# SwiGLU first projections: the seven-product scheme over latent tokens and context together, in halves of 384 tokens

## The chip, the cores and the metric

The kernel runs on one core of a Trainium2 chip. The metric is the device time of one execution in microseconds. A core has a matrix engine (PE, with its weight loads listed apart as PEld), a vector engine (DVE), an activation engine (ACT), a general engine (POOL) and a queue that issues most of the loads (SP).

## The reference, cut to what matters

A trunk of two layers works on 512 latent tokens (x) and 256 context tokens (ctx) of width 1024. Each layer holds two SwiGLU blocks with a mixer between them; the last block of the last layer is done for x alone.

```python
def swiglu(x, w13, w2):
    a, b = jnp.split(x @ w13, 2, axis=-1)          # w13: 1024 x 5632
    return (jax.nn.silu(a) * b) @ w2               # w2: 2816 x 1024
...
    for l in range(DEPTH):
        x = x + 0.5 * ml[2] * swiglu(modulate(x, norm_g[l, 0], ml[0], ml[1]), ffn_w13[l, 0], ffn_w2[l, 0])
        ctx = ctx + 0.5 * mc[2] * swiglu(modulate(ctx, norm_g[l, 0], mc[0], mc[1]), ffn_w13[l, 0], ffn_w2[l, 0])
        ...
        x = x + 0.5 * ml[8] * swiglu(modulate(x, norm_g[l, 2], ml[6], ml[7]), ffn_w13[l, 1], ffn_w2[l, 1])
        if not last:
            ctx = ctx + 0.5 * mc[8] * swiglu(modulate(ctx, norm_g[l, 2], mc[6], mc[7]), ffn_w13[l, 1], ffn_w2[l, 1])
```

## The kernel before, in words

Activations lie transposed, features on the 128 partitions and tokens along the free axis. Every product of the projections is done in split precision: each operand is held as a rounded high part and a low part (`xnhx`, `xnlx` for x, `xnhc`, `xnlc` for the context, `whi`, `wlo` for weights), and `mmk` (L367) issues three matmuls per 128x128 weight tile: high by high (L369), low activation by high weight (L371), high activation by low weight (L373).

There are four SwiGLU blocks, built by `ffn_steps` (L517): f0, f1, f2 for x and context, f3 for x alone. The 2816 hidden features are 22 steps of 128. A plain step (`up`, L559) multiplies eight tiles of the gate half and eight of the value half with 512 columns of x and 256 of the context: 48 matmuls of 512 columns and 48 of 256. Later steps are "fast" ones (`up_fast`, L635): from step 3 on in f0, f2 and f3, from step 18 on in f1, so 19 + 4 + 19 steps with context and 19 without.

A fast step treats the product as a 2x2 block product: the input features in two halves of 512 (four tiles each), the output as gate and value, the 512 tokens of x in two halves of 256. A Strassen-Winograd scheme then needs seven block products (a11, a12, s1, s2, s3, s4, a22) in place of eight, with sums of weight quarters (`fast_job`, L567, on POOL, L576 to L582) and sums of activation quarters. The context takes no part in the scheme: it is multiplied plainly with the four raw quarters a11, a12, a21, a22 of the weights (tile `sc`), which is why a21 is split and kept although the scheme for x does not need it. A step has 7 x 12 matmuls of 256 columns for x and 4 x 12 of 256 for the context.

The activation sums are made once per block by `fast_sums` (L607), called four times (k = 0 to 3) at the places that the tables `FP0` to `FP3` name: in the middle of the first projections of the context, at their end ("e"), or at the end of a given plain step. Per call DVE does seven adds of 256 columns (L615 to L621) and the low part of two sums (L364), POOL three adds and a low part (L612 to L614, L624), ACT the high parts (L363, L623). Sums lie in two tiles `xt0`, `xt1`; the fourth sum `t4` waits in a temporary until `fast_prep2` (L627) writes it over the second half of the lower four tiles of `xnhx`, `xnlx`, just before the first fast step.

Order of the work: each engine runs its instructions in the order in which the program emits them. Weights come by SP into three raw buffers of 2048 columns; `advance` (L128) splits a job into pieces (high part on ACT, L162; low part on DVE, or on POOL for piece s1, L163) as long as fewer than eight pieces are out, and a raw buffer is loaded anew when its last piece has been split. In a fast step each block product gives its piece back by itself (`relc`), and the next piece is split there. The second projections (`down`) come between the fast steps, two steps' features at a time; they add their result to `hT` on DVE (`resid`, L688), which frees the PSUM bank. PSUM has seven banks for products, taken in turn by `PS`.

Of the kernel before, what the change touches and what calls it, by code (L numbers as in the profile page):

```python
# [9 lines left out]
F32 = mybir.dt.float32  # L10
F32R = mybir.dt.float32r
# [3 lines left out]
ALU = mybir.AluOpType  # L15
# [44 lines left out]
def trunk_kernel(  # L60
# [31 lines left out]
    ones = const.tile([P, P], F32, name="ones")  # L92
    nc.vector.memset(ones, 1.0)
# [151 lines left out]
    acc = np_.tile([P, NT + 8], F32, name="acc")  # L245
    rst = np_.tile([P, NT + 8], F32, name="rst")
# [270 lines left out]
    def ffn_steps(l, fi, zf, zt, nxt, parts=PARTS, rest=None, fast=0, prep=(), delay=False):  # L517
# [68 lines left out]
        FORD = ["a11", "a12"] + ["a21"] * both_zs + ["s1", "s2", "s3", "s4", "a22"]  # L586

        def fast_open():
            T["xt"] = tuple(open_pool(f"xt{i}").tile([P, 3, 4, NH], F32R, name=f"xt{i}") for i in range(2))

        def fast_close():
            for i in (1, 0):
                close_pool(f"xt{i}")

        def fast_prep(at):

            for k in [i for i, z in enumerate(prep) if fast and z == at]:
                if k == 0:
                    if (l, fi) == (0, 1):
                        T["drain"]()  # L600
                    fast_open()
                    T["t4"] = [tmp.tile([P, 2, NH], F32, tag="rs_m", name="t4") for _ in range(2)]
                fast_sums(k)

        def fast_sums(k):
            xh, xl = T["xnx"]
            th, tl = T["xt"]  # L607
            q = lambda t, k, h: t[:, k, h * NH:h * NH + NH].bitcast(F32)
            a0, a1, b0, b1 = [(q(xh, k + i, h), q(xl, k + i, h)) for i in (0, 4) for h in range(2)]
            t = tmp.tile([P, SAW], F32, tag="sa", name="tsum")[:, :3 * NH].rearrange("p (i n) -> p i n", i=3)  # L610
            t1, t2, t3, t4 = t[:, 0], t[:, 1], t[:, 2], T["t4"][k // 2][:, k % 2]
# [8 lines left out]
            V.tensor_tensor(t4, b0[0], t2, ALU.subtract)  # L620
            V.tensor_tensor(t4, t4, b0[1], ALU.add)  # L621
            split(th[:, 0:2, k], tl[:, 0:2, k], t[:, 0:2])
            SC.activation(th[:, 2, k], t3, AF.Copy)  # L623
            GP.tensor_tensor(tl[:, 2, k], t3, th[:, 2, k].bitcast(F32), ALU.subtract)  # L624

        def fast_prep2():
            xh, xl = T["xnx"]  # L627
            for i in range(2):
                s = slice(2 * i, 2 * i + 2)
                split(xh[:, s, NH:], xl[:, s, NH:], T["t4"][i])  # L630

        def up_fast(j):
            def fn(w):
                gslot = slot(j)
                xh, xl = T["xnx"]  # L635
                th, tl = T["xt"]
                gh, gl = T["g"]
                s0, s1, s2 = (slice(i * NH, i * NH + NH) for i in range(3))
                pa, pb, pc, pd = (PS(f"s{i}") for i in range(4))
                cc = PS("sc") if both_zs else None  # L640

                def prod(name, ps=None, x=None, half=None, k0=0):

                    wh, wl = w.parts[FORD.index(name)]
                    ws = [(wh[:, hs(k)], wl[:, hs(k)]) for k in range(4)]
                    for k in range(4 if x else 0):
                        mmk([(ps, *x(k))], ws[k], k == 0, k == 3)
                    for k in range(4 if both_zs and half is not None else 0):
                        mmk([(cc[:, half * NCTX:half * NCTX + NCTX], *xk("c", k0 + k))], ws[k], k0 + k == 0, k0 + k == KD - 1)
                    T["relc"](name != "a22")  # L650
                xq = lambda i, s: lambda k: (xh[:, i + k, s], xl[:, i + k, s])
                xt = lambda i: lambda k: (th[:, i, k], tl[:, i, k])
                sa = tmp.tile([P, SAW], F32, tag="sa", name="sa")
                u = tmp.tile([P, NX], F32, tag="rs_m", name="u")
# [5 lines left out]
                prod("a11", pa[:, s0], xq(0, s0), 0)  # L660
                prod("a12", pa[:, s1], xq(4, s0), 0, 4)
                SC.copy(sa[:, s2], pa[:, s0])
                V.tensor_tensor(sa[:, s0], pa[:, s1], sa[:, s2], ALU.add)
                if both_zs:
                    prod("a21", half=1)
                prod("s1", pb[:, s1], xt(0))
                prod("s2", pb[:, s0], xt(1))
                SC.activation(sa[:, s0], sa[:, s0], AF.Silu)
                V.tensor_tensor(u[:, s0], pb[:, s0], sa[:, s2], ALU.add)
                V.tensor_tensor(u[:, s1], pb[:, s1], u[:, s0], ALU.add)  # L670
                prod("s3", pc[:, s1], xt(2))
# [1615 lines left out]
```

## Time and profile before

| | |
|---|---|
| time, median of 3 runs | 2989.99 us (2988.91 to 2992.88) |
| the profiled execution | 2993.55 us |
| its span, first to last instruction | 2991.8 us |
| PE busy | 2832.5 us (95%), 21247 matmuls |
| DVE busy | 2005.1 us (67%) |
| ACT, POOL busy | 1112.4 us (37%), 1087.0 us (36%) |
| mean granted clock of TensorE | 0.963 of full |

Spans count from the first instruction. A busy time counts the union of an engine's instructions; matmuls overlap in the records, so what one costs in a row of many is read from start to start. The block f0 lies at about 65 to 600 us, f1 at about 1330 to 1860, f2 at about 1870 to 2420, f3 at about 2620 to 2980.

### The profile page before, as it was taken

The page shows a single profiled execution, that of the slowest core. Times are in us where ns is not written, and L with a number is a line of the kernel's source. Part 1 is how long each engine was busy: PE and PEld are TensorE (multiplying, and loading weights), DVE is VectorE, ACT ScalarE, POOL GpSimd, SP SyncE. Part 2 cuts the span into 40 slices and gives each one's busy share as a digit, 9 for nine tenths or more (in the row PEclk, how much of TensorE's full clock was granted, in tenths as well). Part 3 has the DMA queues.
Part 4 walks back from the last instruction along what each step waited for, and adds up shares of the span by engine and source line. Part 5 has one row for each costly group of instructions (what it writes and reads, how often), then busy time and mean ns, then how long its engine had stood idle before and what let it go on. Part 6 is the DMA issues. An engine that isn't in the chain of part 4 may idle for free.

```text
span 2991.8 us, 53430 instructions
## 1 busy us (share of the span) xinstructions
PE 2832.5 (95%) x21247; PEld 2520.0 (84%) x21247; DVE 2005.1 (67%) x3817; ACT 1112.4 (37%) x2311; POOL 1087.0 (36%) x1232
## 2 busy tenths in 40 slices
PE   7899999998997899999999999999999989899998
PEld 5799999977885677888888889799999977678997
DVE  4665666667857667658666576766666656588887
ACT  4233333343444435432222233433333332344444
POOL 0242333339307833002655232443333300046653
PEclk9899999998897898999999999999999989899999
DMA  6323341221234584332333211122221226433331
GB/s 228 104 73 127 99 127 57 65 72 43 75 106 158 200 261 150 128 83 76 105 101 103 99 54 54 50 71 62 67 76 60 71 66 211 162 105 100 113 99 64
DMA packets 306104, 308.34 MB, mean 103 GB/s; under 512 B 35053, under 2 KB 261513, under 8 KB 299200
## 3 DMA queue, kind: packets, MB, share of 16 engines
q1 hardware_dynamic: 284592, 274.89, 28.8%
q10 hardware_dynamic: 20256, 25.76, 2.6%
q8 instruction: 167, 2.74, 0.4%
q0 software_dynamic: 1008, 4.29, 0.4%
q14 instruction: 81, 0.66, 0.1%
HBM read 279.34 MB, written 25.56 MB: 102 GB/s over the span
## 4 chain that ended last, share of the span: by engine, by line
PE 73%; DVE 13%; ACT 4%; DMA 2%; POOL 2%; issue 2%; SPq 0%; ACTq 0%; POOLq 0%; DVEq 0%
PE s L369 7%; PE s L373 7%; PE s L371 7%; PE sc L371 3%; PE sc L369 3%; PE sc L373 3%; DVE wlo L163 2%; PE b L1266 1%; DVE nt L321 1%; DVE hT L688 1%; PE uac L373 1%; PE uac L371 1%; PE uac L369 1%; PE uax L369 1%; PE uax L371 1%
## 5 line engine op out<-in xcount | busy, mean ns | idle before, releaser
L163 DVE TENSOR_TENSOR wlo<-raw,whi 128x512 fp32r<-128x512 f32 (+1 forms) x793 | 596.1, 787 | 300.3 <-ACT whi L162 287.5
L162 ACT ACTIVATE whi<-raw 128x512 fp32r<-128x512 f32 (+1 forms) x813 | 476.0, 617 | 687.7 <-PE sc L371 122.4
L369 PE MATMUL s<-xnhx,whi 128*128 128x256 f32 x976 | 277.0, 284 | 0.0
L371 PE MATMUL s<-xnlx,whi 128*128 128x256 f32 x976 | 276.3, 283 | 0.4 <-DVE xnlx L364 0.4
L373 PE MATMUL s<-xnhx,wlo 128*128 128x256 f32 x976 | 276.2, 283 | 0.0
L659 POOL TENSOR_TENSOR gl<-sa,gh 128x256 fp32r<-128x256 f32 x122 | 95.8, 805 | 331.0 <-ACT gh L658 331.0
L373 PE MATMUL s<-xt,wlo 128*128 128x256 f32 x732 | 207.4, 283 | 1.8 <-POOL wlo L163 1.8
L369 PE MATMUL s<-xt,whi 128*128 128x256 f32 x732 | 207.1, 283 | 0.0
L371 PE MATMUL s<-xt,whi 128*128 128x256 f32 x732 | 207.1, 283 | 0.0
L578 POOL TENSOR_TENSOR raw<-raw 128x512 f32<-128x512 f32 x61 | 82.1, 1346 | 311.8 <-issue 286.5
L369 PEld LDWEIGHTS s<-xnhx,whi 128*128 128x128 f32 x976 | 187.2, 192 | 7.6 <-DVE hT L688 3.4
L369 PE MATMUL sc<-xnhc,whi 128*128 128x256 f32 x672 | 190.2, 283 | 0.0
L371 PE MATMUL sc<-xnlc,whi 128*128 128x256 f32 x672 | 190.2, 283 | 0.0
L373 PE MATMUL sc<-xnhc,wlo 128*128 128x256 f32 x672 | 190.1, 283 | 0.0
L371 PEld LDWEIGHTS s<-xnlx,whi 128*128 128x128 f32 x976 | 187.2, 192 | 1.5 <-DVE xnlx L364 0.6
L373 PEld LDWEIGHTS s<-xnhx,wlo 128*128 128x128 f32 x976 | 187.2, 192 | 0.0
L373 PEld LDWEIGHTS s<-xt,wlo 128*128 128x128 f32 x732 | 140.5, 192 | 2.0 <-POOL wlo L163 2.0
L369 PEld LDWEIGHTS s<-xt,whi 128*128 128x128 f32 x732 | 140.5, 192 | 0.0
L371 PEld LDWEIGHTS s<-xt,whi 128*128 128x128 f32 x732 | 140.5, 192 | 0.0
L369 PEld LDWEIGHTS sc<-xnhc,whi 128*128 128x128 f32 x672 | 129.0, 192 | 0.0
L371 PEld LDWEIGHTS sc<-xnlc,whi 128*128 128x128 f32 x672 | 129.0, 192 | 0.0
L373 PEld LDWEIGHTS sc<-xnhc,wlo 128*128 128x128 f32 x672 | 129.0, 192 | 0.0
(760 smaller groups left out, 8403.1 us busy)
## 6 DMA issues: line engine op xcount, KB each, us to landing
raw<-in_ffn_w_dram SPq DMA_DIRECT2D x176, 512.0 KB
raw<-in_w_mod_dram SPq DMA_DIRECT2D x64, 1024.0 KB
raw<-in_ffn_w_dram SPq DMA_DIRECT2D x32, 1024.0 KB
raw<-in_ffn_w_dram SPq DMA_DIRECT2D x16, 768.0 KB
raw<-in_w_mod_dram SPq DMA_DIRECT2D x16, 512.0 KB
raw<-in_e_w_in_dram SPq DMA_DIRECT2D x8, 1024.0 KB
raw<-in_e_w_out_dram SPq DMA_DIRECT2D x8, 1024.0 KB
CAD<-C ACTq DMA_DIRECT2D x4, 1152.0 KB
```

Source lines behind the costliest of these rows:

```text
L162: SC.activation(hi, src, AF.Copy)
L163: (GP if j.slow or c in j.gp else V).tensor_tensor(lo, src, hi.bitcast(F32), ALU.subtract)
L321: V.scalar_tensor_tensor(t, hT[:, k, s], gsc[l][:, i, v, k:k + 1], rst[:, s] if src is None else src, ALU.mult, ALU.mult)
L369: mm(ps, wh, xh, start=first, stop=False)
L371: mm(ps, wh, xl, start=False, stop=False)
L373: mm(ps, wl, xh, start=False, stop=last)
L578: tt(q[2], q[0], q[2], ALU.subtract)
L659: GP.tensor_tensor(gl[:, gslot, s], sa[:, s], gh[:, gslot, s].bitcast(F32), ALU.subtract)
L688: V.scalar_tensor_tensor(hT[:, m, s], ps, ml[:, v, gate * 8 + m:gate * 8 + m + 1], hT[:, m, s], ALU.mult, ALU.add)
L1266: mm(b[q, a + h * 32:a + h * 32 + 32], ch(lhs, h)[q], half(ch(rhs, h)[q], z), start=True, stop=True)
```

## The change

A fast step with context now takes x and context as one row of 768 tokens in two halves of 384: the first half is x[0:384], the second is x[384:512] followed by all of the context. All seven products are done for both; the context's plain products, the piece a21 and the bank `sc` go away. Where a product reads the second half itself (s4 and a22), the half lies in two tiles, and the product is issued as a run of 128 columns and a run of 256 columns into one bank; the other five products have 384 columns. In steps without context the halves stay 256.

Each product has a bank of its own (seven per step in place of five, or four without context). The sums are 384 columns wide; where they read the second half they are done in two pieces. They lie in one tile `xt` of ten sums, and the two that find no room lie in `acc` and `rst`, two tiles of the norms that are idle meanwhile. To make room, the tile `ones` becomes one column that is read 128 times, and the small table `s5c` shares the tile of the convolution weights. `fast_prep2` writes eight pieces in place of two.

```diff
-        FORD = ["a11", "a12"] + ["a21"] * both_zs + ["s1", "s2", "s3", "s4", "a22"]
+        FORD = ["a11", "a12", "s1", "s2", "s3", "s4", "a22"]
+        nh = (NT if both_zs else NX) // 2
+        tail_of = [("x", nh, NX, 0)] + [("c", 0, NCTX, NX - nh)] * both_zs
+        def summed(i, k):
+            n = 4 * i + k
+            if both_zs and n >= 10:
+                t = (acc, rst)[n - 10]
+                return t[:, :nh], t[:, nh:2 * nh]
+            return T["xt"][:, 0, n], T["xt"][:, 1, n]
+        def quarter(i, k, second):
+            r = []
+            for z, c0, c1, o in tail_of if second else [("x", 0, nh, 0)]:
+                hi, lo = T["xn" + z]
+                r.append((o, hi[:, 4 * i + k, c0:c1], lo[:, 4 * i + k, c0:c1]))
+            return r
...
         def fast_sums(k):
-            GP.tensor_tensor(t3, b1[0], a1[0], ALU.subtract)
-            GP.tensor_tensor(t3, t3, b1[1], ALU.add)
-            GP.tensor_tensor(t3, t3, a1[1], ALU.subtract)
-            V.tensor_tensor(t1, a1[0], a0[0], ALU.subtract)
-            V.tensor_tensor(t1, t1, a1[1], ALU.add)
-            V.tensor_tensor(t1, t1, a0[1], ALU.subtract)
-            V.tensor_tensor(t2, b1[0], t1, ALU.subtract)
-            V.tensor_tensor(t2, t2, b1[1], ALU.add)
...
+            for (o, ah, al), (_, bh, bl) in zip(quarter(0, k, True), quarter(1, k, True)):
+                c = slice(o, o + ah.shape[-1])
+                GP.tensor_tensor(t3[:, c], f(bh), f(ah), ALU.subtract)
+                GP.tensor_tensor(t3[:, c], t3[:, c], f(bl), ALU.add)
+                GP.tensor_tensor(t3[:, c], t3[:, c], f(al), ALU.subtract)
+                V.tensor_tensor(t1[:, c], f(ah), f(a0h)[:, c], ALU.subtract)
+                V.tensor_tensor(t1[:, c], t1[:, c], f(al), ALU.add)
+            V.tensor_tensor(t1, t1, f(a0l), ALU.subtract)
+            for o, bh, bl in quarter(1, k, True):
+                c = slice(o, o + bh.shape[-1])
+                V.tensor_tensor(t2[:, c], f(bh), t1[:, c], ALU.subtract)
+                V.tensor_tensor(t2[:, c], t2[:, c], f(bl), ALU.add)
...
         def fast_prep2():
-            for i in range(2):
-                s = slice(2 * i, 2 * i + 2)
-                split(xh[:, s, NH:], xl[:, s, NH:], T["t4"][i])
+            for k in range(4):
+                for o, hi, lo in quarter(0, k, True):
+                    split(hi, lo, T["t4"][k][:, o:o + hi.shape[-1]])
...
+                def prod(name, x):
+                    ps = PS("s")[:, :nh]
                     wh, wl = w.parts[FORD.index(name)]
+                    for i in range(len(x(0))):
+                        for k in range(4):
+                            o, xh, xl = x(k)[i]
+                            mmk([(ps[:, o:o + xh.shape[-1]], xh, xl)], (wh[:, hs(k)], wl[:, hs(k)]), k == 0, k == 3)
...
-                prod("s3", pc[:, s1], xt(2))
-                prod("s4", pc[:, s0], xq(4, s1))
-                V.tensor_tensor(sa[:, NH:3 * NH].rearrange("p (i n) -> p i n", i=2), pc.rearrange("p (i n) -> p i n", i=2),
-                                u[:, s1].unsqueeze(1).to_broadcast([P, 2, NH]), ALU.add)
...
-                if both_zs:
-                    evac("c", gslot, cc[:, :NCTX], cc[:, NCTX:])
+                p7 = prod("s3", xt(2))
+                V.tensor_tensor(u2, p7, u2, ALU.add)
+                p3 = prod("s4", xq(1, True))
+                V.tensor_tensor(sa[:, sB], p3, u1, ALU.add)
+                SC.activation(sa[:, sB], sa[:, sB], AF.Silu)
+                V.tensor_tensor(u1, p7, u1, ALU.add)
+                half(sB, u1)
+                p4 = prod("a22", xq(0, True))
+                V.tensor_tensor(u2, p4, u2, ALU.add)
+                half(sA, u2)
```

How the change moves instructions, at two places. First PE in a fast step with context of f0, in the product a22, where the run over the last tile of x ends and the run over the context begins (`s` is a bank of the scheme, `sc` the context's bank). Before:

```order
L369 MATMUL s_1176<-xnhx,whi_1163 128x256
L371 MATMUL s_1176<-xnlx,whi_1163 128x256
L373 MATMUL s_1176<-xnhx,wlo_1164 128x256
L369 MATMUL sc<-xnhc,whi_1163 128x256
L371 MATMUL sc<-xnlc,whi_1163 128x256
L373 MATMUL sc<-xnhc,wlo_1164 128x256
```

The same piece now (lines 375, 377 and 379 are the three of `mmk`):

```order
L375 MATMUL s<-xnhx,whi_1310 128x128
L377 MATMUL s<-xnlx,whi_1310 128x128
L379 MATMUL s<-xnhx,wlo_1311 128x128
L375 MATMUL s<-xnhc,whi_1310 128x256
L377 MATMUL s<-xnlc,whi_1310 128x256
L379 MATMUL s<-xnhc,wlo_1311 128x256
```

The x part of this product shrinks from 256 to 128 columns with the weight loads as many as before; over the program, 84 matmuls per step stand as 60 of 384, 24 of 256 and 24 of 128 columns, for 132 of 256 before.

Second DVE in the first call of `fast_sums` of f0 (`tsum` holds the sums in work, `t` the fourth sum). Before:

```order
L615 TENSOR_TENSOR tsum<-xnhx 128x256
L616 TENSOR_TENSOR tsum<-tsum,xnlx 128x256
L617 TENSOR_TENSOR tsum<-tsum,xnlx 128x256
L618 TENSOR_TENSOR tsum<-xnhx,tsum 128x256
L619 TENSOR_TENSOR tsum<-tsum,xnlx 128x256
L620 TENSOR_TENSOR t_685<-xnhx,tsum 128x256
L621 TENSOR_TENSOR t_685<-t_685,xnlx 128x256
L364 TENSOR_TENSOR xt_684<-tsum,xt_680 128x2x256
```

The same call now:

```order
L645 TENSOR_TENSOR tsum<-xnhx 128x128
L646 TENSOR_TENSOR tsum<-tsum,xnlx 128x128
L645 TENSOR_TENSOR tsum<-xnhc,xnhx 128x256
L646 TENSOR_TENSOR tsum<-tsum,xnlc 128x256
L647 TENSOR_TENSOR tsum<-tsum,xnlx 128x384
L650 TENSOR_TENSOR tsum<-xnhx,tsum 128x128
L651 TENSOR_TENSOR tsum<-tsum,xnlx 128x128
L650 TENSOR_TENSOR tsum<-xnhc,tsum 128x256
L651 TENSOR_TENSOR tsum<-tsum,xnlc 128x256
L652 TENSOR_TENSOR t_682<-xnhx,tsum 128x384
L653 TENSOR_TENSOR t_682<-t_682,xnlx 128x384
L370 TENSOR_TENSOR xt<-tsum,xt 128x2x384
```

Eight instructions became twelve, at the same place of the queue; on POOL the three adds of a call became six (three of 128, three of 256 columns) and the low part after them 384 columns wide. Nothing else changed its place on either engine there.

## Rows read from the trace of the kernel before

**Rows 1.** The page: chain that ended last, share of the span by engine.

```profile
PE 73%; DVE 13%; ACT 4%; DMA 2%; POOL 2%; issue 2%; SPq 0%; ACTq 0%; POOLq 0%; DVEq 0%
```

**Rows 2.** Timeline of PE in f0 (start, us, engine, line, instruction): one matmul, and the one 132 later.

```profile
149.40 0.28 PE L369 MATMUL s<-xt,whi 128*128 128x256 f32 x1
...
165.24 0.28 PE L369 MATMUL s<-xt,whi 128*128 128x256 f32 x1
```

**Rows 3.** Timeline of PE in f0: a matmul of 512 columns in plain step 2, and the 13th after it.

```profile
89.67 0.39 PE L373 MATMUL ubx<-xnhx,wlo 128*128 128x512 f32 x1
...
92.61 0.28 PE L369 MATMUL uac<-xnhc,whi 128*128 128x256 f32 x1
```

**Rows 4.** Groups by line of one fast step, 149.41 to 165.23 us (xcount | busy us, mean ns | idle before us).

```profile
L371 PE MATMUL sc<-xnlc,whi 128*128 128x256 f32 x17 | 4.8, 283 | 0.0
```

**Rows 5.** Groups of weight loads, whole span, by shape (weights of 128, of 16 columns).

```profile
L369 PEld LDWEIGHTS s<-xnhx,whi 128*128 128x128 f32 x976 | 187.2, 192 | 7.6 <-DVE hT L688 3.4 <-ACT sa L676 2.5 <-issue 0.8
...
L369 PEld LDWEIGHTS pj0x<-xnhx,whi 128*16 128x16 f32 x8 | 0.8, 95 | 0.9
```

**Rows 6.** Timeline of PE at 2484 us: matmuls of 96 columns, weights of 128 columns.

```profile
2484.40 3.81 PE L1913 MATMUL pu<-perm,Ut 96*128 96x96 f32 x32 [0.67 <-ACT Ut L1882]
```

**Rows 7.** Timeline of DVE in f0: starts of the calls, and what follows them.

```profile
81.29 0.41 DVE L615 TENSOR_TENSOR tsum<-xnhx 128x256 f32<-128x256 f32 x1
...
84.98 0.97 DVE L615 TENSOR_TENSOR tsum<-xnhx 128x256 f32<-128x256 f32 x1
...
90.48 0.42 DVE L535 TENSOR_TENSOR sa<-pf,sa 128x256 f32<-128x256 f32 x1
...
92.97 0.97 DVE L615 TENSOR_TENSOR tsum<-xnhx 128x256 f32<-128x256 f32 x1
...
97.63 0.96 DVE L615 TENSOR_TENSOR tsum<-xnhx 128x256 f32<-128x256 f32 x1
...
103.10 2.49 DVE L163 TENSOR_TENSOR wlo<-raw,whi 128x384 fp32r<-128x384 f32 x4
```

**Rows 8.** Groups by shape on DVE and POOL, whole span: prices of 128 and 384 columns.

```profile
L1269 DVE TENSOR_TENSOR wk<-wk,b 128x128 f32<-128x128 f32 x60 | 14.1, 279 | 10.1 <-PE b L1266 9.6
L1937 DVE TENSOR_TENSOR Z<-Z,t__26041 128x384 f32<-128x384 f32 x2 | 1.1, 558 | 0.1
...
L1716 POOL TENSOR_TENSOR Q<-Q,tw 128x128 f32<-128x128 f32 x32 | 16.1, 503 | 2.5
```

**Rows 9.** Timeline of POOL in f0: first and last add of the second call.

```profile
85.63 0.91 POOL L612 TENSOR_TENSOR tsum<-xnhx 128x256 f32<-128x256 f32 x1
...
87.50 0.81 POOL L614 TENSOR_TENSOR tsum<-tsum,xnlx 128x256 f32<-128x256 f32 x1
```

**Rows 10.** Timelines of f0's start: PE; then ACT; then SP's queue.

```profile
112.63 1.87 PE L453 MATMUL modt<-pick,rtmod 128*128 128x4 f32 x8 [12.26 <-ACT rtmod L437]
...
110.35 1.76 ACT L162 ACTIVATE whi<-raw 128x384 fp32r<-128x384 f32 x4 [1.99 <-DMA raw<-in_ffn_w_dram]
112.02 0.56 ACT L437 COPY rtmod<-mod 128x512 f32<-128x512 f32 x1
...
81.86 24.12 SPq L706 DMA_DIRECT2D raw<-in_ffn_w_dram  x2
```

**Rows 11.** Timelines of f1, 1740 to 1756 us: DVE; then PE.

```profile
1740.22 0.42 DVE L535 TENSOR_TENSOR sa<-uac,sa 128x256 f32<-128x256 f32 x1 [1.06 <-ACT sa L534]
...
1754.41 0.86 DVE L688 SCALAR_TENSOR_TENSOR hT<-d0c,modc,hT 128x256 f32<-128x256 f32 x2
...
1755.33 0.80 PE L369 MATMUL d4x<-gh,whi 128*128 128x512 f32 x1 [5.83 <-DVE hT L688]
```

**Rows 12.** Timelines of f2, 1930 to 1941 us: DVE's two runs of down weights; then PE.

```profile
1930.63 2.51 DVE L163 TENSOR_TENSOR wlo<-raw,whi 128x384 fp32r<-128x384 f32 x4
...
1940.94 3.61 DVE L163 TENSOR_TENSOR wlo<-raw,whi 128x384 fp32r<-128x384 f32 x4
...
1930.63 0.50 PE L369 MATMUL d0x<-gh,whi 128*128 128x512 f32 x1 [0.77 <-ACT whi L162]
```

More of the change, by code (lines that the diff above doesn't have):

```diff
@@ L91, in trunk_kernel @@
     make_identity(nc, ident)
-    ones = const.tile([P, P], F32, name="ones")
-    nc.vector.memset(ones, 1.0)
+    one = const.tile([P, 1], F32, name="one")
+    nc.vector.memset(one, 1.0)
+    ones = one.to_broadcast([P, P])
     hT = const.tile([P, KD, NT], F32, name="hT")
@@ L244, in trunk_kernel, with rows_of @@
     tmp = ctx.enter_context(tc.tile_pool(name="tmp", bufs=2))
-    acc = np_.tile([P, NT + 8], F32, name="acc")
-    rst = np_.tile([P, NT + 8], F32, name="rst")
+    acc = rst = None
+    def rows_of(dt):
+        nonlocal acc, rst
+        acc, rst = (np_.tile([P, NT + 8], dt, tag=t, name=t) for t in ("acc", "rst"))
+    rows_of(F32)
     SAW = 888
@@ L585, in fast_job @@
             return job
-        FORD = ["a11", "a12"] + ["a21"] * both_zs + ["s1", "s2", "s3", "s4", "a22"]
+        FORD = ["a11", "a12", "s1", "s2", "s3", "s4", "a22"]
+        nh = (NT if both_zs else NX) // 2
+        tail_of = [("x", nh, NX, 0)] + [("c", 0, NCTX, NX - nh)] * both_zs
         def fast_open():
-            T["xt"] = tuple(open_pool(f"xt{i}").tile([P, 3, 4, NH], F32R, name=f"xt{i}") for i in range(2))
+            n = 10 if both_zs else 12
+            T["xt"] = open_pool("xt").tile([P, 2, n, nh], F32R, name="xt")
+            T["t4"] = {}
+            rows_of(F32R)
         def fast_close():
-            for i in (1, 0):
-                close_pool(f"xt{i}")
+            close_pool("xt")
+            rows_of(F32)
+        def summed(i, k):
[10 more added lines that the diff above has]
+            return r
         def fast_prep(at):
@@ L601, in fast_prep @@
                     fast_open()
-                    T["t4"] = [tmp.tile([P, 2, NH], F32, tag="rs_m", name="t4") for _ in range(2)]
+                T["t4"][k] = tmp.tile([P, NX], F32, tag="rs_m" if k < 2 else "sq", name="t4")[:, :nh]
                 fast_sums(k)
         def fast_sums(k):
[L606 to L609, printed above, removed]
@@ L618, in fast_sums @@
-            V.tensor_tensor(t2, b1[0], t1, ALU.subtract)
-            V.tensor_tensor(t2, t2, b1[1], ALU.add)
[L620 to L624, printed above, removed]
+            f = lambda a: a.bitcast(F32)
+            (_, a0h, a0l), = quarter(0, k, False)
@@ new lines, in fast_sums @@
+            V.tensor_tensor(t1, t1, f(a0l), ALU.subtract)
[3 more added lines that the diff above has]
+                V.tensor_tensor(t2[:, c], t2[:, c], f(bl), ALU.add)
+            V.tensor_tensor(t4, f(b0h), t2, ALU.subtract)
+            V.tensor_tensor(t4, t4, f(b0l), ALU.add)
+            xt = T["xt"]
+            split(xt[:, 0, k:k + 5:4], xt[:, 1, k:k + 5:4], t)
@@ L634, in fn @@
                 gslot = slot(j)
-                xh, xl = T["xnx"]
-                th, tl = T["xt"]
                 gh, gl = T["g"]
[L638 to L642, printed above, removed]
+                sA, sB = slice(0, nh), slice(nh, 2 * nh)
+                def prod(name, x):
+                    ps = PS("s")[:, :nh]
                     wh, wl = w.parts[FORD.index(name)]
[L645 to L652, printed above, removed]
+                    for i in range(len(x(0))):
+                        for k in range(4):
+                            o, xh, xl = x(k)[i]
+                            mmk([(ps[:, o:o + xh.shape[-1]], xh, xl)], (wh[:, hs(k)], wl[:, hs(k)]), k == 0, k == 3)
+                    T["relc"](name != FORD[-1])
+                    return ps
+                xq = lambda i, second: lambda k: quarter(i, k, second)
+                xt = lambda i: lambda k: [(0, *summed(i, k))]
                 sa = tmp.tile([P, SAW], F32, tag="sa", name="sa")
-                u = tmp.tile([P, NX], F32, tag="rs_m", name="u")
+                u2 = tmp.tile([P, NX], F32, tag="rs_m", name="u2")[:, :nh]
+                u1 = tmp.tile([P, NX], F32, tag="sq", name="u1")[:, :nh]
                 def half(s, b):
@@ L1549, in trunk_kernel @@
     MD = dram.tile([4, 8, 16, 240], F32, name="MD")
-    s5c = const.tile([P, 32], F32, name="s5c")
+    s5c = cwT[:, 0:32]
     class Later:
```

36 lines of the change are left out of this document (16 added, 20 removed).

## The prediction, as it was put on record

> **What bounds the kernel now.** I read the page's chain first: 73% of it is PE and 13% DVE [rows 1]. So PE sets most of the time, but a stretch in which DVE is late counts too. Then one fast step on PE's timeline. A matmul starts at 149.40 us, and the one 132 later, which begins the same product of the next step, at 165.24 [rows 2]: 15.84 us, 0.120 us for each of the 132 matmuls of 256 columns. The groups of that step show no idle time before a matmul [rows 4]. So in the fast steps PE is the bound with nothing to spare, and whatever the change saves or adds on PE per step comes out in full, 42 times (the steps with context); faster splitting of weights there earns nothing.
>
> Last I read the places where PE does wait near the sums of the activations. In f0 it waits 12.26 us before `modt`, for a copy on ACT [rows 10]; in f1 5.83 us before `d4x`, for DVE's additions to `hT` [rows 11]; in f2 0.77 us before `d0x`, for a split of weights [rows 12]. All three are waits for work queued behind `fast_sums`.
>
> **The change on PE.** A step with context loses 132 matmuls of 256 columns (15.84 us) and gets 60 of 384, 24 of 256 and 24 of 128. In columns that is 33792 against 32256, 4.5% less; but a matmul does not cost its columns alone. 256 columns take 0.120 us [rows 2] and 512 take 0.226, 2.94 us for 13 [rows 3]: a line of 0.014 us plus 0.000414 per column. On it 384 columns cost 0.173 us; the 60 make 10.38 us, and the 24 of 256 make 2.88.
>
> The 128-column matmul is the disputed price: no split product here is that short. The line gives 0.067 us. But each brings a load of 128 weight columns. The record of such a load is 192 ns, that of one of 16 columns 95 [rows 5]: 97 ns for 112 columns, so 128 columns keep the load path busy for some 111 ns (an estimate from these two rows). With 256 columns in flight this hides; with 128 it cannot. The nearest matmuls with a short moving side are the 32 of L1913, 96 columns on 128 weight columns: 3.81 us from first start to last end, and less the last one's own 0.28 us that is 0.114 us from start to start [rows 6]. I take 0.114, because the operand that I think decides has the same size there. The ends for the range are 0.067 and 0.120 (no dearer than twice the columns).
>
> 24 x 0.114 = 2.74, so a step takes 10.38 + 2.88 + 2.74 = 16.00 us, 0.16 more than now: 42 x 0.16 = **+6.7 us**. The ends are 42 x (14.87 - 15.84) = -40.7 and 42 x (16.14 - 15.84) = +12.6. The arithmetic saving is eaten by cutting the second half in two.
>
> **The change in the sums.** One call of `fast_sums` on DVE takes 84.98 - 81.29 = 3.69 us where POOL leaves it alone [rows 7]: seven adds of 256 columns, 0.46 from start to start, and a low part. Now it has four adds of 128 columns (0.28, so 0.32 with the step between two), four of 256 (0.46), three of 384 (0.56, so 0.59) [rows 8], and a low part of 768 columns, about 0.86 on the slope of 128, 256 and 384: 1.28 + 1.84 + 1.77 + 0.86 = 5.75, **+2.06 a call**. The second call takes 90.48 - 84.98 = 5.50 and the third 4.66 [rows 7]; they overlap POOL's three adds (85.63 to 88.31 [rows 9]), and DVE's adds then take twice as long. So 1.81 and 0.97 us of these calls are the overlap. POOL's three adds of 0.8 become three of 0.8 and three of 0.5 [rows 8, 9], 3.9 us for 2.7, and I scale the overlap by 1.45: the second and fourth call grow by 2.06 + 0.81 = 2.87, the third by 2.06 + 0.44 = 2.5.
>
> Does anything hide it? In **f0** no: DVE goes straight from the fourth call to the down weights at 103.10 [rows 7]; these free the raw buffer for which SP's queue has waited 24.12 us; the load lands, ACT splits at 110.35, and only then does ACT copy the row for which PE waits [rows 10]. All four calls shift that: 2.06 + 2.87 + 2.5 + 2.87 = +10.3. In **f1** two calls lie behind each of steps 16 and 17, and PE, out of banks, already waits for the DVE work behind the last: 2 x (2.06 + 2.87) = 9.9, less the 1.06 us that DVE still idles between [rows 11]: +8.8. In **f2** three calls come before the split at 1930.63 for which PE waits: +7.4. The fourth comes between the two runs of splits, 10.3 us apart [rows 12]; the 36 matmuls of 512 and 36 of 256 columns that PE does meanwhile take 12.5 us, and 10.3 + 2.5 = 12.8 is near enough: 0. In **f3** the halves stay 256: 0. Together **+26.5 us**; the ends are 12 (half hidden) and 36 (a DVE that must follow POOL's seven instructions a call).
>
> **The rest.** At the end of f0, f1 and f2 the last hidden features pass through two DVE operations, one on ACT and one on POOL that are 384 wide: some 0.6 us longer, **+1.8**. `fast_prep2` writes eight pieces for two; the weights for about one step are split ahead, so 0. One weight piece in eight less per step saves DVE 0.6 us and ACT as much, the evacuation's nine instructions of 384 give back about as much, and PE waits for neither: 0; uncovered it would be a few tenths per step. The raw loads keep their order on SP. Seven banks per step for seven in all: each is read a whole step before its next use, 0. `ones`, `s5c`, `acc` and `rst` are idle when they are lent: 0.
>
> Sum: 6.7 + 26.5 + 1.8 = +35.0 us. On the profiled execution's 2993.55 that is 3028.6; that execution is 3.6 us above the median of the runs shown, 2989.99, so I forecast **3025 us**. Differences of 0.2% (6 us) or less I take as not measurable.
>
> **The rivals.**
> - *The short matmul costs its columns.* If weight loads overlap better than the rows of L1913 suggest, the 128-column matmul falls on the line: -40.7 + 28.3 = -12.4, 2978 us, faster. For it: the line fits 256 and 512. Against it: the load's record and the 0.114 us of a matmul shorter still. It decides below a price of 0.079 us, where 42 x (13.26 + 24 x price - 15.84) meets -28.3; from 0.073 to 0.085 the result cannot be told from no change.
> - The Trainium skill, page "TensorE: Matmul & The Clock Gate", section "Back-to-back issue gap", speaks for this rival: it gives about 81 ns per matmul for a stream of pairs of weight load and 128-column matmul, by which the sum would be about 2992. No pair of split products that short runs here, and L1913's are slower.
> - *The sums hide better.* If PE's waits at the three places have another cause that ends as late (the load in f0 held up by its own traffic, say), only a third of the 26.5 shows: 6.7 + 8.8 + 1.8 = +17, 3007 us. For it: SP's queue waits in f0. Against: its wait ends when DVE's and ACT's splits free the buffer.
> - *The fast steps lose their cover.* POOL makes four weight sums, a split and two low parts per step, the last two now half as wide again; if a piece comes late once per step by 0.5 us, 42 x 0.5 = +21: 3046 us. Against: one step on POOL comes to under 10 of 16 us.
>
> **How the numbers follow.** The forecast gets 0.60, the sums hidden 0.12, lost cover 0.10, the cheap short matmul 0.11, and a price between, which gives no change, 0.07. The forecast's own range is 3010 to 3037 (prices of PE and sums not all at one end); with most of the hidden-sums case and the nearer part of lost cover it becomes 2995 to 3050. Slower by over 0.2% holds 0.60 + 0.12 + 0.10, which I put at 0.81; faster 0.12; same 0.07.
>
> **What would show it.** In PE's timeline the 128-column matmuls of s4 and a22 should start 0.11 to 0.12 us apart, the 384-column ones 0.173, with a step of 16.0 us and still no idle time in it. The calls of `fast_sums` should take 5.7 us alone and 7 to 8.5 beside POOL; PE should wait over 20 us before `modt` in f0, some 14 before `d4x` in f1 and some 8 before `d0x` in f2. A step near 14.9 us would make the forecast wrong in sign; waits before these three as now would make it too high.

## The result, and the profile after

The changed kernel takes **3040.98 us** (median of 5 runs, 3039.78 to 3045.09) against 2989.99 for the kernel before (5 runs beside it): ratio **1.0174, 95% interval 1.0160 to 1.0188**. It is 51 us slower. The forecast was 3025 with 2995 to 3050: direction and range held, the size was 16 us short.

The profiled execution took 3045.09 us. From its page, the span and the engines' busy time (share of the span), with instruction counts:

```profile
span 3043.3 us, 51689 instructions
...
PE 2844.4 (93%) x20239; PEld 2529.6 (83%) x20239; DVE 2089.7 (69%) x3820; ACT 1087.5 (36%) x2205; POOL 1167.3 (38%) x1268
```

PE has 1008 matmuls fewer (24 in each of 42 steps) and is still busy 12 us longer. The first look is at PE's timeline in f0 (start, us, engine, line, instruction), the counterpart of [rows 2]: the first matmul of a fast step, the twelve of 128 columns in s4 with their neighbours, and the first matmul of the next step.

```profile
155.51 0.33 PE L375 MATMUL s<-xnhx,whi 128*128 128x384 f32 x1
...
165.93 0.22 PE L375 MATMUL s<-xnhx,whi 128*128 128x128 f32 x1
165.99 0.28 PE L377 MATMUL s<-xnlx,whi 128*128 128x128 f32 x1
166.10 0.27 PE L379 MATMUL s<-xnhx,wlo 128*128 128x128 f32 x1
...
167.11 0.28 PE L379 MATMUL s<-xnhx,wlo 128*128 128x128 f32 x1
167.22 0.33 PE L375 MATMUL s<-xnhc,whi 128*128 128x256 f32 x1
167.39 0.28 PE L377 MATMUL s<-xnlc,whi 128*128 128x256 f32 x1
...
171.49 0.34 PE L375 MATMUL s<-xnhx,whi 128*128 128x384 f32 x1
```

A step takes 171.49 - 155.51 = 15.98 us where it took 15.84 [rows 2]. Of the short matmuls the first takes its place 0.06 us long, the others 0.11 (165.99, 166.10, ... 167.11, 167.22). So matmuls with half the columns of the old ones cost almost what the old ones did (0.120). The granted clock is 1.00 of full in this stretch.

The second look is at what PE waits for in the three stretches of [rows 10], [rows 11] and [rows 12] (us in total, times, longest); the last row is DVE's longest wait in the stretch of f1.

```profile
PE modt L459 <- ACT rtmod L443: 24.3, 1, 24.3
...
PE d4x L375 <- DVE hT L715: 18.4, 1, 18.4
...
PE d0x L375 <- ACT whi L163: 9.8, 1, 9.8
...
DVE wlo L164 <- ACT whi L163: 3.2, 1, 3.2
```

PE's three were 12.26, 5.83 and 0.77. The third look is at DVE behind these waits: in f0 the starts of the four calls of `fast_sums` and the splits that follow, in f1 the last two calls and what follows.

```profile
84.18 0.28 DVE L645 TENSOR_TENSOR tsum<-xnhx 128x128 f32<-128x128 f32 x1
...
89.70 1.00 DVE L645 TENSOR_TENSOR tsum<-xnhx 128x128 f32<-128x128 f32 x1
...
101.88 0.43 DVE L645 TENSOR_TENSOR tsum<-xnhx 128x128 f32<-128x128 f32 x1
...
108.77 0.97 DVE L645 TENSOR_TENSOR tsum<-xnhx 128x128 f32<-128x128 f32 x1
...
116.62 4.88 DVE L164 TENSOR_TENSOR wlo<-raw,whi 128x384 fp32r<-128x384 f32 x4
...
1765.01 0.43 DVE L645 TENSOR_TENSOR tsum<-xnhx 128x128 f32<-128x128 f32 x1
...
1766.57 0.84 DVE L646 TENSOR_TENSOR tsum<-tsum,xnlc 128x256 f32<-128x256 f32 x1
...
1771.95 0.96 DVE L645 TENSOR_TENSOR tsum<-xnhx 128x128 f32<-128x128 f32 x1
...
1779.80 3.16 DVE L164 TENSOR_TENSOR wlo<-raw,whi 128x512 fp32r<-128x512 f32 x2
1786.12 1.08 DVE L164 TENSOR_TENSOR wlo<-raw,whi 128x512 fp32r<-128x512 f32 x1 [3.15 <-ACT whi L163]
1787.12 0.86 DVE L715 SCALAR_TENSOR_TENSOR hT<-d0c,modc,hT 128x256 f32<-128x256 f32 x2
```

In f0 the stretch from the first call to the splits is 116.62 - 84.18 = 32.4 us, against 21.8 [rows 7]: +10.6. The calls are as long as forecast: 5.52 alone, 6.89 and 7.85 beside POOL. But the four splits behind them, 2.49 us before [rows 7], now take 4.88. In f1 the two calls take 14.8 us, and between them and the additions to `hT` lie 7.3 us of three weight splits and a wait (1779.80 to 1787.12). In the kernel before, three splits stand there too, without that wait, and 3.3 us after their start the additions begin (1754.41 [rows 11]):

```profile
1751.09 3.40 DVE L163 TENSOR_TENSOR wlo<-raw,whi 128x512 fp32r<-128x512 f32 x3
```

POOL's timeline of the changed kernel there shows why:

```profile
1779.20 1.54 POOL L658 TENSOR_TENSOR rst<-tsum,rst 128x384 fp32r<-128x384 f32 x1 [1.65 <-ACT rst L657]
1780.71 1.70 POOL L582 TENSOR_TENSOR s<-raw 128x512 f32<-128x512 f32 x1
1782.49 1.59 POOL L584 TENSOR_TENSOR raw<-raw 128x512 f32<-128x512 f32 x1
1784.16 1.26 POOL L585 TENSOR_TENSOR raw<-s,raw 128x512 f32<-128x512 f32 x1
```

The low part of the last call (L658) holds back the weight sums of the first fast step (L582 to L585); ACT's high part and DVE's split of that sum wait for them; and the additions to `hT`, for which PE waits, are queued on DVE behind that split.

To add up, I followed the same instructions on PE through both traces; the difference of the spans is 51.5 us. Start before f0: +1.9. Waits around the three places: +12.0 in f0, +12.6 in f1, +11.7 in f2 (9.1 before the first `d0x`, 1.5 in the `d` products after it, 1.0 in the second half): **+36.3**. The 42 fast steps: **+5.6**. Tails of f0, f1, f2: +1.2. Mixer of layer 0: +3.7. Between f2 and f3: +1.4. f3: +1.0. Together 51.1.

The 1.5 us in f2 are no wait. Behind the 9.8 us in which PE stood idle, its granted clock is 0.50 of full, the 1.2 GHz level; in the same products of the kernel before it is 1.00. The rows are two matmuls of 512 columns, then a window (its length; busy time and count of PE, PEld, DVE, ACT, POOL; granted clock; DMA), first of the changed kernel, then of the kernel before.

```profile
1976.36 0.63 PE L377 MATMUL d1x<-gl,whi 128*128 128x512 f32 x1
1976.79 0.63 PE L379 MATMUL d1x<-gh,wlo 128*128 128x512 f32 x1
1974.00:1979.00 5.00, 4.58 (x11) 3.09 (x11) 4.30 (x8) 2.39 (x6) 1.04 (x2) 0.50 0.17 49
...
1932.36 0.40 PE L371 MATMUL d1x<-gl,whi 128*128 128x512 f32 x1
1932.59 0.40 PE L373 MATMUL d1x<-gh,wlo 128*128 128x512 f32 x1
1931.00:1936.00 5.00, 4.27 (x17) 2.68 (x16) 3.82 (x8) 2.62 (x6) 1.06 (x2) 1.00 0.30 86
```

From start to start that is 0.43 us against 0.23. In f0 and f1 both kernels have such a stretch behind the wait: 7.6 us before and 6.5 now in f0, 3.3 and 3.8 in f1.

### The profile page after: what moved, and what is told of

Same layout as the page of the kernel before. It is cut to its first block, busy times and chain, and to the rows that moved or that the text cites. A ratio compares the mean times of both kernels' runs of the same rounds, so it can differ in the third digit from the quotient of the medians.

```text
span 3043.3 us, 51689 instructions
## 1 busy us (share of the span) xinstructions
PE 2844.4 (93%) x20239; PEld 2529.6 (83%) x20239; DVE 2089.7 (69%) x3820; ACT 1087.5 (36%) x2205; POOL 1167.3 (38%) x1268
## 3 DMA queue, kind: packets, MB, share of 16 engines
q0 software_dynamic: 1008, 4.29, 0.4%
## 5 line engine op out<-in xcount | busy, mean ns | idle before, releaser
L163 ACT ACTIVATE whi<-raw 128x512 fp32r<-128x512 f32 (+2 forms) x771 | 448.2, 616 | 676.1 <-PE s L377 197.2
L377 PE MATMUL s<-xnlx,whi 128*128 128x384 f32 (+1 forms) x976 | 291.6, 299 | 1.0 <-DVE xnlx L370 1.0
L379 PE MATMUL s<-xnhx,wlo 128*128 128x384 f32 (+1 forms) x976 | 290.8, 298 | 0.0
L375 PE MATMUL s<-xnhx,whi 128*128 128x384 f32 (+1 forms) x976 | 287.2, 294 | 0.0
L690 POOL TENSOR_TENSOR gl<-sa,gh 128x384 fp32r<-128x384 f32 (+1 forms) x122 | 122.8, 1023 | 314.3 <-ACT gh L689 314.3
L585 POOL TENSOR_TENSOR raw<-s,raw 128x512 f32<-128x512 f32 x61 | 93.8, 1538 | 318.1 <-DVE wlo L164 290.3
L375 PE MATMUL s<-xt,whi 128*128 128x384 f32 (+1 forms) x648 | 205.7, 317 | 3.9 <-DVE u L698 3.9
L379 PE MATMUL s<-xt,wlo 128*128 128x384 f32 (+1 forms) x648 | 205.5, 317 | 0.0
L377 PE MATMUL s<-xt,whi 128*128 128x384 f32 (+1 forms) x648 | 205.4, 317 | 0.0
L582 POOL TENSOR_TENSOR s<-raw 128x512 f32<-128x512 f32 x61 | 90.8, 1489 | 98.7 <-DMA raw<-in_ffn_w_dram 98.7
L375 PE MATMUL s<-xnhc,whi 128*128 128x256 f32 x336 | 99.3, 296 | 0.0
L379 PE MATMUL s<-xnhc,wlo 128*128 128x256 f32 x336 | 95.0, 283 | 0.0
```

Of the source, the lines that this page charges most:

```text
L163: SC.activation(hi, src, AF.Copy)
L375: mm(ps, wh, xh, start=first, stop=False)
L377: mm(ps, wh, xl, start=False, stop=False)
L379: mm(ps, wl, xh, start=False, stop=last)
L582: tt(job.s1, q[2], q[3], ALU.add)
L585: tt(q[0], job.s1, q[0], ALU.subtract)
```

## The experiments

**Theory 1:** two terms make the time: the split second half costs PE a weight load per short matmul, which eats what the scheme saves; and the wider sums come out in full at the three places. **Rivals:** the small edits (`ones`, `s5c`) or other places hold part of it; the calls only stand in the wrong places. Each ratio below is to the kernel before, run on the same chip.

### The second half in one run

```diff
-  p3 = prod("s4", xq(1, True))
-  p4 = prod("a22", xq(0, True))
+  p3 = prod("s4", xt(2) if both_zs else xq(1, True))
+  p4 = prod("a22", xt(0) if both_zs else xq(0, True))
```

> The changed kernel, but s4 and a22 of the steps with context read a sum of 384 columns in one run (s3's and s1's operand) in place of the second half in runs of 128 and 256; it leaves out those two products' own operand, so its values differ, and it has 12 matmuls fewer per product. Theory 1 (the runs of 128 columns cost a weight load, 0.112 us each): each of the 24 pairs, 0.112 + 0.120 us, becomes one matmul of 0.173, so a step falls from 15.97 to 14.56 us, 42 x 1.41 = 59 us less: about 2982 us, with no idle time in PE's steps. Theory 2 (the step is held by the pieces of weights from ACT, DVE and POOL as soon as PE is faster): the step stays above 15.3 us with waits of PE for splits, and the time stays above 3010.

Measured: **2984.43 us**, ratio 0.9977 (0.9965 to 0.9988). First matmul of a step and of the next, on PE's timeline:

```profile
155.46 0.33 PE L375 MATMUL s<-xnhx,whi 128*128 128x384 f32 x1
...
170.06 0.33 PE L375 MATMUL s<-xnhx,whi 128*128 128x384 f32 x1
```

The step is 14.60 us, 1.38 less than in the changed kernel; 42 x 1.38 = 58 us, and the time fell by 56.6. The waits at the three places stayed (24.2, 18.4, 9.8). So the split half costs some 56 us, more than the 51 by which the change is slower; without it, and without what a whole row would cost to make, the kernel is 0.2% faster than the one before.

### Sums without low parts, and the small edits alone

e2 leaves the low parts of the operands out of the sums in context blocks: six of DVE's eleven adds in a call and four of POOL's six.

```diff
-  GP.tensor_tensor(t3[:, c], t3[:, c], f(bl), ALU.add)
-  V.tensor_tensor(t1[:, c], t1[:, c], f(al), ALU.add)
-  V.tensor_tensor(t4, t4, f(b0l), ALU.add)
...
```

> The changed kernel, but in the blocks with context fast_sums leaves out every addition of a low part: DVE has 6 instructions per call for 12, POOL 3 for 7 (values differ slightly). Theory 1 (PE's waits before modt in f0, before d4x in f1 and before d0x in f2 are DVE's queue behind these calls): a call takes about 3.0 us alone for 5.5 and 4 beside POOL for 7.9, f0 falls by 14 us, f1 by 12 to 16, f2 by 9 to 11, together 36 to 40: about 3003 us; PE's wait before modt in f0 is near 10 us for 24, before d4x in f1 near 4 for 18, before d0x in f2 near 0 for 10. Theory 2 (the waits are set by the raw loads and POOL's weight sums): less than 15 us in all, above 3025.

Measured: **3003.22 us**, ratio 1.0042 (1.0026 to 1.0058). PE's waits: 9.6 before `modt`, 7.8 before `d4x`, none before `d0x`. So these adds are worth about 38 us, and the three waits go with them. In f1 some 8 us were left where 4 were expected: a call is not all that stands ahead of `hT`.

e3 is the kernel before with the column `ones` and with `s5c` in `cwT`:

```diff
-  ones = const.tile([P, P], F32, name="ones")
+  one = const.tile([P, 1], F32, name="one")
+  ones = one.to_broadcast([P, P])
-  s5c = const.tile([P, 32], F32, name="s5c")
+  s5c = cwT[:, 0:32]
```

> The kernel before with only the two edits that make room: ones as a column read 128 times, s5c in the tile of the convolution weights. Theory 1 (the 3.7 us by which the mixer of layer 0 and the 1.9 us by which the start came out longer are scatter between executions): 2990 us within 6, and the mixer of layer 0 as long as before within a few us either way. Theory 2 (the edits add waits there): 2993 to 2996, with a mixer longer by 3 to 4 us and new waits at lines that read ones or cwT.

Measured: **2997.52 us**, ratio 1.0021 (1.0011 to 1.0031): the two edits cost 3 to 9 us, and the time lies above both expected ranges. The profiled execution, 2993.83 us, is among the fastest of the eight, and its span of 2992.1 is only 0.3 above that of before, so this trace doesn't hold the whole difference. One part of it is plain from all traces: the first matmul into `pf` starts at 30.1 to 30.8 us in the three kernels without the edits (before, e7, e10) and at 32.1 to 32.7 in all eleven with them. The mixer, +3.7 in the changed kernel, scatters instead: from the last products of f0 to the first `pf` of f1 it is 661.0 us in the changed kernel, 654.9 in e3 and 658.4 in e2, which do the same there, and 656.6 to 662.7 in the three without the edits. Where the rest of the 3 to 9 us lies stays open.

### Other places for the calls

e4 is the changed kernel with the calls spread, and fast steps from 5 on in f0 and f2 to make room:

```diff
-  NDIR = (3, 18, 3, 3)
-  FP0 = [(1, 4), (1, 7), "e", "e"];  FP1 = [16, 16, 17, 17];  FP2 = [(1, 4), (1, 7), "e", 2]
+  NDIR = (5, 18, 5, 3)
+  FP0 = ["e", 2, 3, 4];  FP1 = [14, 15, 16, 17];  FP2 = ["e", 2, 3, 4]
```

> The changed kernel with the four sum calls spread: in f0 and f2 at the end of the first projections and of plain steps 2, 3 and 4, with fast steps from 5 on (two plain steps more each, 16.6 us for 15.97), in f1 at steps 14 to 17. Theory 1 (the calls cost only where DVE has no idle time behind them; a plain step has some 11 us of it): f0 loses 18 to 22 us of PE's wait, f1 15 to 18, f2 9 to 11, and four plain steps cost 2.5: 3041 - 40 + 2.5, about 3000 us, between 2993 and 3012. Theory 2 (the calls only move the delay to the next split of weights): above 3025.

Measured: **3013.08 us**, ratio 1.0077 (1.0058 to 1.0097): 28 us came back, 13 fewer than expected and 1 us outside the range. The wait before `modt` fell to 6.9, but with a call just ahead of the first fast step that step is 5 us longer in f0 and f2 (waits of 2.1 and 0.7 us for the sums, then matmuls at a granted clock of 0.50), and in f1 5.7 us before `d4x` stayed.

### The second half copied into whole rows

e5 leaves nothing out: after the last sum, ACT and DVE copy the split halves into rows of 384 columns (in the rooms of x and context that are read no more), so that 21 of the 24 pairs of runs in a step become one matmul.

```diff
+  for k in range(4):
+      (_, _, dh, dl), = second(1, k)
+      for o, hi, lo in quarter(1, k, True):
+          n = hi.shape[-1]
+          SC.activation(dh[:, o:o + n], hi.bitcast(F32), AF.Copy)
+          V.tensor_copy(dl[:, o:o + n], lo.bitcast(F32))
...
```

> The changed kernel with the second half put together: before the first fast step of a block with context, ACT and DVE copy its upper four tiles into rows of 384 columns in the context's tile, and fast_prep2 writes the new lower four into what is free by then, so that 21 of the 24 pairs of runs become one matmul of 384 columns. Nothing is left out. Theory 1 (the short runs are what eats the saving): a step takes 81 x 0.173 + 3 x 0.232 = 14.7 us for 15.97, 42 x 1.27 = 53 us less, and the copies are hidden or cost up to 3 us a block: 2988 to 2997 us, about the kernel before, with the waits before modt, d4x and d0x as in the changed kernel. Theory 2 (rows with strides and copies cost as much as the runs saved): above 3020.

Measured: **2993.46 us**, ratio 1.0015 (1.0004 to 1.0027), 47.5 us below the changed kernel and as expected.

```profile
156.25 0.33 PE L375 MATMUL s<-xnhx,whi 128*128 128x384 f32 x1
...
170.96 0.39 PE L375 MATMUL s<-xnhx,whi 128*128 128x384 f32 x1
```

The step is 14.71 us, 1.13 below that of before, and all three waits are as in the changed kernel. What the steps save against the kernel before, 42 x 1.13 = 47 us, is eaten up: 36 go with the sums, the rest with the other terms above and the copies.

e6 adds spread calls (as e4, with the last call of f0 and f2 moved to step 3, those of f1 after 13 to 16), e7 gives the kernel before the same tables:

```diff
+  NDIR = (5, 18, 5, 3)
+  FP0 = ["e", 2, 3, 3];  FP1 = [13, 14, 15, 16];  FP2 = ["e", 2, 3, 3]
```

> The same with the calls of fast_sums spread (f0 and f2: at the end of the first projections, of plain step 2, and two at step 3, fast from step 5; f1: at steps 13 to 16). Theory 1 (both costs are separate and add): 2990 less some 30 to 38 of waits, and four plain steps of 16.6 us for 14.7 cost 7.6 us: 2955 to 2970 us, faster than both kernels by 0.7 to 1.2%. Theory 2 (with steps of 14.7 us DVE and POOL have no idle time left for the calls): above 2985.

> The kernel before with the same spread tables. It says how much of the last gain belongs to the place of the calls and not to the change. Theory 1 (its calls are shorter, 3.7 to 5.5 us, and PE waits 21 us for them in all): it gains 8 to 15 us of waits and loses 4 x 0.8 = 3 us to plain steps: 2977 to 2988. Theory 2 (the places were right for its calls): 2988 to 3000.

Measured: e6 **2978.17 us**, ratio 0.9958 (0.9940 to 0.9976), 8 us above its expected range; e7 **2996.23 us**, ratio 1.0016 (1.0004 to 1.0028), as the rival said. Both readings have the same flaw, which the waits of PE between 1600 and 1660 us in e6 show:

```profile
PE pm L1860 <- DVE C L1769: 9.4, 1, 9.4
...
PE pq L1819 <- POOL Q L1769: 2.8, 1, 2.8
```

(e7 has 9.6 and 2.8.) The first call of f1 empties the side work of the mixer that is still pending (`T["drain"]()` in `fast_prep`); after step 13 some 60 small operations on DVE and 50 on POOL are left of it, which now run in one go with PE waiting, about 20 us in e6 and 16 in e7.

### The calls of f1 one step later

```diff
-  FP1 = [13, 14, 15, 16]
+  FP1 = [14, 15, 15, 16]
```

> The kernel of e6_whole_spread with the four calls in f1 after steps 14, 15, 15 and 16 in place of 13 to 16; all is computed. Theory 1: e6 lost about 20 us in f1 at 1622 to 1650 us, because its first call empties the mixer's pending side work at one place (pq waits 2.8 for POOL, pm 9.4 for DVE's chain of 60 small operations); one step later that work has run out by itself. Then 2978.2 less about 18: 2960 us (2954 to 2968). Theory 2: the wait comes from the calls' own load on DVE; then two calls after step 15 bring it back: 2970 to 2982.

> The kernel before with the tables of e9: fast steps from 5, 18, 5 and 3, calls after steps e, 2, 3, 3 in f0 and f2, after 14, 15, 15, 16 in f1. It is the counterpart that shows what the places alone are worth without wide products. Theory 1: e7 (2996.2) held the same loss in f1, there about 15.6 us, so that its reading said nothing on the places: 2981 us (2975 to 2987), below the kernel before. Theory 2: the places of the kernel before were the best for its shorter calls: 2990 to 3000.

Measured: e9 **2970.08 us**, ratio 0.9925 (0.9911 to 0.9939); e10 **2985.32 us**, ratio 0.9971 (0.9960 to 0.9982). The waits for the side work are gone from both, so the verdict of e7 is withdrawn: spread calls help the kernel before too, by 0.3%. e10 came out as expected; e9 lies 2 us above its range, at the edge of its rival's. Of the 18 us that it should have gained on e6 it gives more than half back, in f1:

```profile
PE d4x L375 <- DVE hT L741: 11.0, 1, 11.0
```

Right behind step 15 stand the second projections; the additions to `hT` that free their banks queue on DVE behind the two calls. At equal places the wide products with whole rows are worth 2985.32 - 2970.08 = 15 us, of the 38 x 1.13 = 43 us that the steps save. Part of the difference stands in the waits before `modt` and `d4x`: 6.9 and 11.0 us in e9, 5.3 and 5.0 in e10.

e11 takes the calls of f0 to steps 2, 3, 4, 4 with fast steps from 6 on; e12 takes those of f1 to 14, 14, 16, 16.

> The kernel of e9 with fast steps in f0 from 6 on and its calls after steps 2, 3, 4, 4: none is left ahead of modt. Theory 1: the 6.9 us wait before modt goes, one fast step less costs about 1.9 us: 5 us below e9 (about 2955). Theory 2: the two calls after step 4 hold the steps after them by as much: no difference to e9, within 3 us.

> The kernel of e9_whole_late with the calls in f1 after steps 14, 14, 16 and 16, so that none is left after step 15 or 17, right behind which the second projections stand, whose hT adds queue on DVE behind the calls. Theory 1: what counts is which work stands next on DVE, not how many calls follow each other: the 11.2 us wait of PE's d4c/d4x group in f1 goes, and nothing takes its place, since the step that follows two calls (16.6 us of PE) covers about 15 us of them: 2970 less 11, 2959 us (2953 to 2965). Theory 2: two calls in a row are too much for DVE wherever they stand: the wait moves and the time stays, 2966 to 2975.

Measured: e11 **2970.91 us**, ratio 0.9930 (0.9915 to 0.9945); e12 **2968.55 us**, ratio 0.9919 (0.9906 to 0.9933). Both as their rivals said: no difference to e9. In e11 the wait before `modt` is 6.9 us as in e9, with no call ahead of it, so the call there did not make it; a fast step fewer costs 1.9, and 2 us stand before each of two groups of `d4x`. In e12 the 11.0 us went, and these came, between 1660 and 1760 us:

```profile
PE d0c L375 <- ACT whi L163: 2.8, 1, 2.8
PE d4x L375 <- DVE hT L741: 2.5, 1, 2.5
PE d0c L379 <- DVE wlo L164: 1.1, 1, 1.1
```

Now the weight splits are late (ACT's high part, DVE's low part) in place of `hT`. In these versions what is late changes with the place; that something is late does not. e9, e11 and e12, which cannot be told apart, are the fastest versions found: 0.7 to 0.8% below the kernel before, 2.4% below the changed one.

### The calls without their POOL work

What was still open was why the sums came out 10 us above the forecast. e8 is the changed kernel; in blocks with context it leaves out the fifth sum and its low part on POOL, and ACT copies one of the sum's operands in their place:

```diff
-  GP.tensor_tensor(t3[:, c], f(bh), f(ah), ALU.subtract)
-  GP.tensor_tensor(t3[:, c], t3[:, c], f(bl), ALU.add)
-  GP.tensor_tensor(t3[:, c], t3[:, c], f(al), ALU.subtract)
...
-  GP.tensor_tensor(lo, t3, f(hi), ALU.subtract)
+  SC.activation(hi, f(b0h), AF.Copy)
+  SC.activation(lo, f(b0l), AF.Copy)
```

> The changed kernel, in which the calls of fast_sums in context blocks make no POOL work: the fifth sum (three or six adds and a low part on POOL) is left out, and ACT writes one of its operands, high and low, in its place. DVE's part of the calls is untouched. Theory 1: the term of the sums came out near 36 us where 26.5 were forecast because DVE's adds run at about half speed beside POOL's, and because POOL's longer sums stand ahead of the weight sums and so make the weight splits on DVE late. Then four calls in f0 cost DVE about 4 x 5.6 in place of 32.4, PE's wait before modt falls from 24.3 to about 12, the one before d4x from 18.4 to about 8, the one before d0x from 9.8 to under 3: some 28 us together, 3013 us (3008 to 3019). Theory 2: DVE's own longer adds set the wait and POOL's share is small: the three waits fall by under 8 us together, 3033 us or more.

Measured: **3012.48 us**, ratio 1.0068 (1.0049 to 1.0088): 28.5 us less, as theory 1 said. PE's waits in the three stretches:

```profile
PE modt L459 <- ACT rtmod L443: 12.3, 1, 12.3
...
PE d4x L375 <- DVE hT L720: 8.2, 1, 8.2
...
PE d0x L375 <- ACT whi L163: 4.8, 1, 4.8
```

And DVE's timeline in f1, the same two calls and splits as above:

```profile
1748.51 0.29 DVE L646 TENSOR_TENSOR tsum<-xnhx 128x128 f32<-128x128 f32 x1
...
1749.49 0.42 DVE L647 TENSOR_TENSOR tsum<-tsum,xnlc 128x256 f32<-128x256 f32 x1
...
1753.92 0.28 DVE L646 TENSOR_TENSOR tsum<-xnhx 128x128 f32<-128x128 f32 x1
...
1759.62 1.29 DVE L164 TENSOR_TENSOR wlo<-raw,whi 128x512 fp32r<-128x512 f32 x2 [0.20 <-ACT whi L163]
1762.73 1.08 DVE L164 TENSOR_TENSOR wlo<-raw,whi 128x512 fp32r<-128x512 f32 x1 [1.81 <-ACT whi L163]
```

DVE's work in a call is untouched, and yet a call falls from 7 or 8 us to 5.41 (1748.51 to 1753.92). The same add of 256 columns takes 0.42 us where it took 0.84, and two splits take 1.29 us where they took 3.16. In f0 the four splits behind the calls take 1.96 us, against 2.49 before and 4.88 in the changed kernel. The wait in f0 is the one of before, to the tenth, but by two effects that cancel: DVE's part is longer than before, and POOL's is gone. The third wait kept 4.8 us, where under 3 were expected. The run takes away POOL's old share together with the new one, and doesn't tell how much of the old waits POOL's shorter sums made in the kernel before; that was not tried.

## Why the prediction was right in sign and short in size

- **PE in the fast steps: right.** The forecast priced the short matmul at 0.114 us from a row of another part [rows 6], against 0.067 on the line through the longer ones. The trace has 0.11 for all but the first of a run; the step came to 15.98 for 16.00, the term to +5.6 for +6.7. e1 shows what hung on it: 56 us, more than the change lost.
- For that price the forecast took the matmuls of 96 columns as the nearest. The trace of the kernel before has nearer ones: `qs`, 128 columns on 128 weight columns, and `modth`, 4 columns on as many, both at a granted clock of 1.00:

```profile
22.91 1.06 PE L475 MATMUL modth<-pick,rtmod0h 128*128 128x4 f32 x8 [0.70 <-ACT rtmod0h L437]
...
1024.61 2.05 PE L1302 MATMUL qs<-S,qkT 128*128 128x128 f32 x16
```

  Less the last one's own 0.25 and 0.28 us that is 0.116 us from start to start for 4 columns and 0.118 for 128. So the moving columns do not set the price in this range. That the load of the weights sets it, and no other cost of a matmul on a full weight tile, is argued and not shown: the matmuls `py`, with 128 moving columns but only 64 weight columns, also start 0.11 us apart (four from 2499.22 on take 0.60 us, less the last one's 0.27).
- The rival of the cheap short matmul fell with it, and the figure of the Trainium skill that spoke for it (page "TensorE: Matmul & The Clock Gate", section "Back-to-back issue gap", about 81 ns) does not hold for these products. The same page's "LDWEIGHTS (loading the stationary operand)" gives a load's time as its columns over 1.2 per ns, by which 128 columns take 107 ns. The eleven short matmuls behind the first of a run take 167.22 - 165.99 = 1.23 us here, 112 ns each, 5 ns more than that.
- **The sums: the term that was mis-sized**, 26.5 forecast and 36.3 measured. Its places were right, and so was the length of the calls in f0 (+10.6 for +10.3). Wrong was to price the calls and nothing beside them: "All four calls shift that" left the splits around them at their old price, and they took 4.88 us for 2.49 beside POOL's low part and weight sums. In f1 the forecast of +8.8 held for the calls, and 4 us came on top, because POOL's low part delays the weight sums, these delay the splits, and `hT` queues behind the splits. In f2 it was 11.7 for 7.4: the wait before `d0x` grew by 9.1, the fourth call, "near enough: 0", cost 1.0, and 1.5 went with the granted clock of 0.50 behind the longer wait, for which the forecast has no term. The waits were to be over 20, some 14 and some 8 us; they are 24.3, 18.4 and 9.8.
- e8 shows a common cause of these waits: DVE is slower beside POOL and waits for what POOL has delayed, and 28 us of the changed kernel's time go with POOL's share. How the 9.8 us above the forecast divide between POOL's longer part and DVE's is not shown, as POOL's old share went with it. The measured 36.3 lies at the forecast's upper end of 36, which was set for a DVE that must follow POOL; with the clock and the fourth call in it, so close a match is partly luck.
- **The tails:** +1.2 for +1.8.
- **Nothing was forecast** for the start (+1.9), the mixer (+3.7), the stretch before f3 (+1.4) and f3 (+1.0). The start goes with the small edits: "idle when they are lent: 0" held for the room, but the edits are not free, 3 to 9 us in e3's runs. The mixer scatters, and so does the stretch before f3 (139 to 144 us over the traces).
- **The other rivals:** the sums hide nowhere: the waits shrink as soon as the calls get shorter (e2, e8), so no other cause held PE as long. The fast steps did not lose their cover: between the matmuls of three steps in f0 no idle time stands.

Short of the forecast by 16: 9.8 from the sums, 8.0 from places not forecast, less 1.7 from steps and tails.

## What to carry to other kernels

In a run of matmuls on full 128x128 weight tiles each took at least 0.11 us here, all but the first, however few its columns. So where a scheme saves columns by cutting a matmul in two short ones, price the pieces from rows of that shape: here the saving went, and it was cheaper to copy the operand into one row once per block (e5: 47.5 us) than to read it in pieces in every step. When you widen work on one engine, price its neighbours too: the instructions that the other engine runs beside it, what is queued behind it on the way to the busiest engine, and the clock that this engine has after a longer wait. Compare two versions each with places that suit it, and look in the trace for what a moved call triggers before you believe that a place was bad.

## What was not expected of the hardware

- In a run of twelve matmuls of 128 columns the first takes 0.06 us, what its columns alone would cost on the line, and the first of 256 columns behind the run 0.17 instead of 0.12. It looks as if the load hides behind the matmul ahead of it and the short ones have no room for it; no run here separates the load from the matmul.
- DVE's add of 256 columns takes 0.42 us alone and 0.84 in the same place beside POOL's adds; four splits of weights take 2.49 us or 4.88. The Trainium skill (page "SBUF — State Buffer", section "Who interferes with whom") says that an instruction of DVE with two inputs in SBUF contends with one of POOL that reads SBUF. Both kinds here have two such inputs, and e8 agrees: with POOL's adds gone the same instructions are back at 0.42. POOL is slowed too: its add of 256 columns takes 0.74 us while DVE is idle (1741.69 in the changed kernel) and up to 1.05 beside DVE's adds (1753.03).
